# A LoRA residual kernel: the first eight tiles become two parts, and the seventh load waits for TensorE

## The chip, the cores and the metric

The kernel runs on one core of a Trainium2 chip. The metric is the device time of one execution in microseconds; the time of a kernel is the median of several executions. The kernel before takes 123.56 us (three runs, 123.53 to 123.73).

## The reference

```python
# x: (16, 512, 768) float32, A: (768, 16), B: (16, 768), scale = 0.5
lora = np.matmul(np.matmul(x, A), B)
return (x + scale * lora).astype(np.float32)
```

The rows of x are 16 * 512 = 8192 tokens of 768 numbers. Each token is projected to 16 numbers, these are raised to 768 again, scaled and added to the token. About 25 MB are read and 25 MB written.

## The kernel before, in words

**Tiles and parts.** A tile is 128 tokens, one on each of the 128 partitions of the on-chip memory: 128 rows of 3072 B, 384 KB. There are 64 tiles. `PARTS` (L14) cuts them into five parts of 8, 8, 16, 16 and 16 tiles. Within a part of S tiles, partition p holds S tokens that follow each other in memory (`memory`, L96 to L98). A transfer of all S tiles of a part is one run of memory, and each partition's piece of it is S * 3072 B long; a transfer of some of a part's tiles takes a piece out of every S * 3072 B. `x_sb` has room for 48 tiles (`ROOM`, L61), so tiles 48 to 63 take the places of tiles 0 to 15 once those have been stored (`tiles`, L103).

**Groups.** The engines work in eight groups of 8 tiles (`GROUP`). For each group:

1. ScalarE narrows tiles 0 to 3 of the group to fp16 and GpSimd tiles 4 to 7 (`narrowed`, L186 to L196, into `xn`). The first group is cut finer: tiles 0 and 1 go to GpSimd, 2 and 3 and then 4 to 7 to ScalarE. Each waits for the load that holds its tiles.
2. VectorE transposes 32x32 blocks (`turned`, L248, into `xt`).
3. TensorE projects the group with 24 matmuls (`projected`, L278 to L291, `MMS` = 24, into `ps_yt`).
4. ScalarE copies and scales the projection into a block diagonal `y_bd` (L236 to L239).
5. TensorE raises pairs of tiles (`raised`, L293 to L310, into `lora_ps`), and VectorE adds each pair to x in place (`summed`, L252 to L259, line L255, into `x_sb`).

TensorE runs a loop over the groups: raised(0), raised(1) of group g, the first 12 matmuls of the projection of group g+1, raised(2), raised(3) of group g, the last 12 matmuls of the projection. ScalarE narrows its half of group g+1 ahead of copying the projection of group g.

**SyncE issues every transfer, in an order written out by hand** (`on_sync`, L135 to L182), all on one DMA queue:

- loads 0 and 1 (tiles 0 and 1, then 2 to 7, both pieces of the first part of 8), A in three pieces, B, then loads 2 to 5 (tiles 8 to 47);
- a wait until groups 0 and 1 are summed and until the tenth pair has been raised (`s_lora`, L169); then store 0 (tiles 0 to 7) and store 1 (tiles 8 to 15), L170 and L171;
- a wait until store 0 has landed (L172), then load 6 (tiles 48 to 55, into the places of 0 to 7); a wait until store 1 has landed (L174), then load 7 (tiles 56 to 63);
- for each of the last three parts of 16 tiles a wait for its sums, then its store. The first of these also waits for the sixth group's first raise (`s_raise`, L181).

A DMA over 128 partitions has 16 engines to run on. It counts its semaphore up by 16 when it has landed, 1 for each engine that is done. `STORES` (L128) lists the stores, and `STORED` (L130) the group after which each may go.

Of the kernel before, what the change touches and what calls it, by code (L numbers as in the profile page):

```python
# [10 lines left out]

PARTS = [8, 8, 16, 16, 16]  # L14


GROUP = 8
# [11 lines left out]
def kernel(  # L29
# [8 lines left out]
    nc = tc.nc  # L38
# [9 lines left out]
    NC = D // 64  # L48
    NG = sum(PARTS) // GROUP
    PAIRS = GROUP // 2  # L50
    assert sum(PARTS) * P == T and NG * GROUP == sum(PARTS)
    sc = float(scale)


    def sb(name, shape, dtype):
        return nc.alloc_sbuf_tensor(name, shape, dtype).ap()
# [3 lines left out]

    ROOM = sum(PARTS[:-1])  # L61
    x_all = sb("x_sb", [P, ROOM, D], fp32)
# [20 lines left out]
    def sem(name):  # L83
        sems.append(nc.alloc_semaphore(name))
        return sems[-1]
# [4 lines left out]
    tok = 0  # L90
    for i, S in enumerate(PARTS):
        parts.append(tok)
# [3 lines left out]
    def memory(t2, i, s, n):  # L96
        S = PARTS[i]
        return t2[ds(parts[i], S * P), :].rearrange("(p s) d -> p s d", s=S)[:, ds(s, n), :]  # L98

    def held(i, s, n):  # L100
        return tiles(where.index((i, s)), n)

    def tiles(t, n):  # L103
        return x_all[:, ds(t % ROOM, n), :]

    LOADS = [
        (0, 0, 2), (0, 2, 6), (1, 0, 8), (2, 0, 8), (2, 8, 8), (3, 0, 16), (4, 0, 8), (4, 8, 8)
    ]
    s_load = [sem(f"s_load{k}") for k in range(len(LOADS))]

# [10 lines left out]

    s_free = [sem(f"s_free{p}") for p in range(PAIRS)]
    s_out0, s_out1, s_raise = sem("s_out0"), sem("s_out1"), sem("s_raise")

    s_sum, s_out = sem("s_sum"), sem("s_out")

    MMS = 2 * NC
    STORES = [(0, 0, 8), (1, 0, 8), (2, 0, 16), (3, 0, 16), (4, 0, 16)]  # L128

    STORED = [where.index((i, s + n - 1)) // GROUP for i, s, n in STORES]  # L130

    section = ExitStack()
    section.enter_context(tc.tile_critical(no_gpsimd_drain=True))  # L133

    def on_sync(e):  # L135
        def load(k):
            ld = LOADS[k]
            e.dma_start(out=held(*ld), in_=memory(x2, *ld)).then_inc(s_load[k], 16)  # L138

        def summed(k):  # L140
            e.wait_ge(s_sum, k + 1)
            if STORED[k] + 1 < NG:

                e.sem_inc(s_free[PAIRS - 1], 1)

        def store(k, done):
            st = STORES[k]
            e.dma_start(out=memory(out2, *st), in_=held(*st)).then_inc(done, 16)

        load(0)  # L150
        load(1)
        e.wait_ge(s_ready, 1)
        blocks = A.rearrange("(c e) r -> c (e r)", e=64)
        for c in range(SETS):
            e.dma_start(
                out=a_rows[c : SET * SET : SET, :], in_=blocks[ds(c * SET, SET), :]
            ).then_inc(s_a, 16)
        e.wait_ge(s_brows, 1)
        e.dma_start(out=b_rows[0 : R * APART : APART, :], in_=B).then_inc(s_b, 16)
        for k in range(2, len(LOADS) - 2):  # L160
            load(k)

        for p in range(2, PAIRS):
            e.sem_inc(s_free[p], 1)
        summed(0)
        summed(1)


        e.wait_ge(s_lora, 2 * PAIRS + 2)  # L169
        store(0, s_out0)  # L170
        store(1, s_out1)  # L171
        e.wait_ge(s_out0, 16)  # L172
        load(len(LOADS) - 2)
        e.wait_ge(s_out1, 16)  # L174
        load(len(LOADS) - 1)
        for k in range(2, len(STORES)):
            summed(k)
            if k == 2:


                e.wait_ge(s_raise, 6)  # L181
            store(k, s_out)  # L182

    here = set()

# [55 lines left out]
    def on_vector(e):  # L241
# [10 lines left out]
        def summed(g, p):  # L252
            xs = tiles(g * GROUP + 2 * p, 2)
            e.wait_ge(s_lora, g * PAIRS + p + 1)
            ins = e.tensor_tensor(out=xs, in0=xs, in1=lora[p % 2], op=mybir.AluOpType.add)  # L255
            if p + 1 == PAIRS and g in STORED:
                ins.then_inc(s_sum, 1)
# [15 lines left out]
    def on_tensor(e):  # L273


        xv = xt.rearrange("p s (c j k) -> p s c j k", c=NC, k=2)

        def projected(first, last):  # L278
            for m in range(first, last):
                c, k = divmod(m, 2)  # L280
                mm = e.matmul(  # L281
                    y_ps, w_bd[:, c, k, :], xv[:, :, c, :, k],
                    start=(m == 0), stop=(m == MMS - 1),
                )
                if m == 0:
                    mm.then_inc(s_turned, -1)
                if m == 1:

                    mm.then_inc(s_taken, 1)
                if m == MMS - 1:  # L290
                    mm.then_inc(s_y, 1)  # L291

        def raised(p):  # L293
            if p == 0:
                e.wait_ge(s_spread, 1)
            free = s_free[(p + 2) % PAIRS]
            e.wait_ge(free, 1)
            t = lora[p % 2]
            mms = []
            for k in range(2):  # L300
                for n0, w in ((0, 512), (512, 256)) if k == 0 else ((0, 256), (256, 512)):
                    mms.append(e.matmul(  # L302
                        t[:, k, ds(n0, w)], y_bd[:, 2 * p + k, :], b_mm[:, ds(n0, w)],
                        start=True, stop=True,
                    ))
            if p == 0:
                mms[0].then_inc(s_raise, 1)
                mms[2].then_inc(s_spread, -1)
            mms[1].then_inc(free, -1)
            mms[-1].then_inc(s_lora, 1)  # L310

        e.wait_ge(s_pick, 2)
        e.wait_ge(s_bh, 1)
        for n0, w in ((0, 512), (512, 256)):
            last = e.matmul(  # L315
                lora[0][:, 0, ds(n0, w)], pick.rearrange("p b r -> p (b r)"),
                b_half[:, ds(n0, w)], start=True, stop=True,
            )
        last.then_inc(s_bp, 1)
        e.wait_ge(s_w, 1 + NQ)  # L320
        e.wait_ge(s_turned, 1)
        projected(0, MMS)
        e.wait_ge(s_bm, 1)
        with e.Fori(0, NG - 1):
            raised(0)
            raised(1)
            e.wait_ge(s_turned, 1)
            projected(0, MMS // 2)
            raised(2)
            raised(3)  # L330
            projected(MMS // 2, MMS)
        for p in range(PAIRS):
            raised(p)

    on_sync(nc.sync)
    on_gpsimd(nc.gpsimd)
    on_scalar(nc.scalar)
# [5 lines left out]

    nc.gpsimd.wait_ge(s_sum, len(STORED))
    nc.gpsimd.sem_clear(range(nums[0], s_sum.num))
    nc.gpsimd.wait_ge(s_out, (len(STORES) - 2) * 16)
    nc.gpsimd.sem_clear(range(s_sum.num, s_out.num + 1))
    section.close()

# [34 lines left out]
```

## Time and profile before

| what | value |
|---|---|
| median of three runs | 123.56 us |
| the profiled execution: its time | 123.76 us |
| its span, from the first to the last instruction | 121.9 us |
| outside the span | 1.9 us |
| DMA queue: packets' time as a share of 16 engines' span | 96.8% |
| busy: VectorE, TensorE, ScalarE, GpSimd | 81.7, 50.5, 37.4, 28.4 us |
| read and written | 25.26 and 25.17 MB, 414 GB/s over the span |

The page cuts the span into 40 slices of 3.05 us. Its line "DMA" gives the mean busy share of the 16 DMA engines in each slice, in tenths, and its line "GB/s" what they moved. A transfer stands three times in the trace: as the instruction of SyncE that issues it, as the packets that its engines move (start, length and size of each), and as the 16 counts of its semaphore, called its landing here. One packet is one partition's piece of a transfer: 3072 B for each tile in it. Landings show how far the 16 engines are apart. Packets don't name their engine.

### The profile page before, as it was taken

The numbers are of one execution on the slowest core, as the hardware profiler recorded it, in microseconds if no ns is written. First come the engines' busy times: TensorE is split into PE (matmuls) and PEld (weight loads), VectorE is DVE, ScalarE is ACT, GpSimd is POOL, SyncE is SP. The second block draws the span as 40 slices with busy tenths as digits, with TensorE's granted clock in tenths as the row PEclk, the third lists the DMA queues.
The fourth block names the chain that finished last, engine by engine and source line by source line (L and its number), as shares of the span: only waits on it lengthen the run. The fifth ranks groups of instructions, "written<-read, shape, count | busy, mean of one in ns | idle before, by whom it ended". The sixth has DMA issues, their size and how long they took to land.

```text
span 121.9 us, 885 instructions
## 1 busy us (share of the span) xinstructions
PE 50.5 (41%) x322; PEld 29.3 (24%) x322; DVE 81.7 (67%) x42; ACT 37.4 (31%) x43; POOL 28.4 (23%) x24
## 2 busy tenths in 40 slices
PE   0000239487457457647756714774674320000000
PEld 0000026244233233424424402442442110000000
DVE  0003850799999999999999959999995991000000
ACT  4003929444426402917230093643004000000000
POOL 7732638044026002607100090630000000000000
PEclk9999999999999999999999999999999985555555
DMA  3999999999997996999989999998998999899890
GB/s 67 421 429 429 443 443 403 451 435 419 476 516 339 435 516 298 460 403 443 443 363 460 427 427 468 451 484 387 419 500 387 403 516 403 371 516 419 355 516 0
DMA packets 1928, 50.43 MB, mean 414 GB/s; under 512 B 236, under 2 KB 236, under 8 KB 392
## 3 DMA queue, kind: packets, MB, share of 16 engines
q1 hardware_dynamic: 1928, 50.43, 96.8%
HBM read 25.26 MB, written 25.17 MB: 414 GB/s over the span
## 4 chain that ended last, share of the span: by engine, by line
DVE 33%; DMA 29%; PE 9%; ACT 6%; POOL 2%; issue 2%; SPq 0%; DVEq 0%
DVE x_sb L255 21%; DMA x_sb<-in_x_dram 20%; DVE xt L250 12%; DMA out_dram<-x_sb 9%; PE ps_yt L281 6%; ACT xn L194 3%; PE lora_ps L302 3%; ACT y_bd L238 2%; POOL xn L194 2%; SPq L138 0%; SPq L379 0%; DVEq L268 0%; SPq L133 0%
## 5 line engine op out<-in xcount | busy, mean ns | idle before, releaser
L255 DVE TENSOR_TENSOR x_sb<-x_sb,lora_ps 128x1536 f32<-128x1536 f32 x32 | 53.7, 1735 | 1.4 <-PE lora_ps L302 1.4
L302 PE MATMUL lora_ps<-b_mm,y_bd 128*128 128x512 f16 (+1 forms) x128 | 25.1, 328 | 23.7 <-ACT y_bd L238 15.3
L194 ACT CAST xn<-x_sb 128x3072 f16<-128x3072 f32 (+1 forms) x9 | 23.4, 2609 | 37.2 <-DMA x_sb<-in_x_dram 28.0
L250 DVE STREAM_TRANSPOSE xt<-xn 128x3072 f32<-128x3072 f32 (+1 forms) x9 | 27.0, 3005 | 6.7 <-PE ps_yt L281 4.9
L194 POOL CAST xn<-x_sb 128x3072 f16<-128x3072 f32 (+1 forms) x8 | 20.7, 2588 | 45.3 <-DMA x_sb<-in_x_dram 28.6
L281 PE MATMUL ps_yt<-xt,w_bd 128*128 128x256 f16 x192 | 25.7, 285 | 11.9 <-DVE xt L250 11.9
L281 PEld LDWEIGHTS ps_yt<-xt,w_bd 128*128 128x128 f16 x192 | 18.7, 100 | 19.6 <-issue 15.0
L302 PEld LDWEIGHTS lora_ps<-b_mm,y_bd 128*128 128x128 f16 x128 | 10.5, 97 | 36.8 <-ACT y_bd L238 17.5
L238 ACT ACTIVATE y_bd<-ps_yt 32x256 f16<-32x256 f32 x32 | 12.0, 374 | 17.7 <-PE ps_yt L281 17.4
L243 DVE STREAM_TRANSPOSE a_t<-a_rows 32x1024 f32<-32x1024 f32 x1 | 1.9, 1945 | 11.2 <-DMA a_rows<-in_A_dram 11.2
L315 PE MATMUL lora_ps<-b_half,pick 128*128 128x512 f16 (+1 forms) x2 | 0.8, 500 | 12.5 <-POOL b_half L212 12.5
L315 PEld LDWEIGHTS lora_ps<-b_half,pick 128*128 128x128 f16 x2 | 0.1, 105 | 12.5 <-issue 12.5
L220 POOL COPY w_bd<-w_one 32x384 f16<-32x384 f16 x4 | 2.0, 501 | 0.2
L212 POOL CAST b_half<-b_rows 128x768 f16<-128x768 f32 x1 | 0.8, 830 | 4.5 <-DMA b_rows<-in_B_dram 4.5
L194 ACT ACT_TABLE_LOAD x1 | 1.3, 1283 | 0.9 <-SPq L133 0.9
L202 POOL MEMSET w_bd<- 128x1536 f32 x1 | 1.4, 1372 | 0.0
L199 POOL MEMSET a_rows<- 32x1024 f32 x1 | 0.9, 941 | 0.5 <-SPq L133 0.5
L214 POOL CAST w_one<-a_t 32x384 f16<-32x384 f32 x1 | 0.8, 847 | 0.9 <-DVE a_t L243 0.9
L231 ACT CAST b_mm<-lora_ps 128x768 f16<-128x768 f32 x1 | 0.8, 798 | 0.0
L200 POOL MEMSET b_rows<- 128x768 f32 x1 | 0.7, 727 | 0.0
L203 POOL MEMSET y_bd<- 128x512 f32 x1 | 0.5, 514 | 0.0
L205 POOL TENSOR_SCALAR_AFFINE_SELECT pick<-pick 128x128 f16<-128x128 f16 x1 | 0.3, 300 | 0.0
(5 smaller groups left out, 0.6 us busy)
## 6 DMA issues: line engine op xcount, KB each, us to landing
out_dram<-x_sb SPq DMA_DIRECT2D x3, 6144.0 KB, 20.0
x_sb<-in_x_dram SPq DMA_DIRECT2D x5, 3072.0 KB, 14.8
x_sb<-in_x_dram SPq DMA_DIRECT2D x1, 6144.0 KB, 41.9
out_dram<-x_sb SPq DMA_DIRECT2D x2, 3072.0 KB, 14.9
x_sb<-in_x_dram SPq DMA_DIRECT2D x1, 2304.0 KB, 9.7
x_sb<-in_x_dram SPq DMA_DIRECT2D x1, 768.0 KB, 4.5
a_rows<-in_A_dram SPq DMA_DIRECT2D x3, 16.0 KB
b_rows<-in_B_dram SPq DMA_DIRECT2D x1, 48.0 KB, 7.4
```

What stands on the lines that cost most here:

```text
L194: ins = copy(out=xn[:, ds(first, n), :], in_=tiles(t, n))
L199: e.memset(a_rows[0:Q], 0.0).then_inc(s_ready, 1)
L202: e.memset(w_bd.rearrange("p c k m -> p (c k m)").bitcast(fp32), 0.0)
L212: e.tensor_copy(out=b_half, in_=b_rows).then_inc(s_bh, 1)
L220: e.tensor_copy(out=w_bd[ds(b * Q, Q), :, :, ds(b * Q, R)], in_=w_one).then_inc(s_w, 1)
L238: last = e.mul(out=y_bd[q, :, q], in_=y_ps[q, :, :], mul=sc)
L243: e.transpose(out=a_t[0:Q].rearrange("i k r c -> i (k r) c"), in_=a_rows[0:Q].rearrange("c (i k r) -> c (k r) i", k=2, r=R),).then_inc(s_r ...
L250: return e.transpose(out=ts[0], in_=ts[1])
L255: ins = e.tensor_tensor(out=xs, in0=xs, in1=lora[p % 2], op=mybir.AluOpType.add)
L281: mm = e.matmul(y_ps, w_bd[:, c, k, :], xv[:, :, c, :, k], start=(m == 0), stop=(m == MMS - 1),)
L302: mms.append(e.matmul(t[:, k, ds(n0, w)], y_bd[:, 2 * p + k, :], b_mm[:, ds(n0, w)], start=True, stop=True,))
L315: last = e.matmul(lora[0][:, 0, ds(n0, w)], pick.rearrange("p b r -> p (b r)"), b_half[:, ds(n0, w)], start=True, stop=True,)
```

## The change

The first part of 8 tiles becomes two parts of 2 and 6 tiles, so that each of the first two loads is one run of memory and not 128 pieces out of a longer one. Tokens 0 to 255 are then tiles 0 and 1, and tokens 256 to 1023 are tiles 2 to 7. The store of 8 tiles becomes two: the 6 tiles first, then the 2, both counting one semaphore to 32. Load 6 waits for both, and then also for a new semaphore, `s_part`, to reach 5: TensorE counts it up at the twenty-first of the 24 matmuls of every projection (m == 20), so it reaches 5 near the end of the fifth group's projection. The rest of the order, and the instructions of all engines but SyncE, stay as they are; the lists are renumbered for the added part.

```diff
-PARTS = [8, 8, 16, 16, 16]
+PARTS = [2, 6, 8, 16, 16, 16]
...
     LOADS = [
-        (0, 0, 2), (0, 2, 6), (1, 0, 8), (2, 0, 8), (2, 8, 8), (3, 0, 16), (4, 0, 8), (4, 8, 8)
+        (0, 0, 2), (1, 0, 6), (2, 0, 8), (3, 0, 8), (3, 8, 8), (4, 0, 16), (5, 0, 8), (5, 8, 8)
     ]
...
-    STORES = [(0, 0, 8), (1, 0, 8), (2, 0, 16), (3, 0, 16), (4, 0, 16)]
+    STORES = [(1, 0, 6), (0, 0, 2), (2, 0, 8), (3, 0, 16), (4, 0, 16), (5, 0, 16)]
     STORED = [where.index((i, s + n - 1)) // GROUP for i, s, n in STORES]
+    assert STORED[0] == STORED[1]
+    STORED = STORED[1:]
...
         e.wait_ge(s_lora, 2 * PAIRS + 2)
         store(0, s_out0)
-        store(1, s_out1)
-        e.wait_ge(s_out0, 16)
+        store(1, s_out0)
+        store(2, s_out1)
+        e.wait_ge(s_out0, 32)
+        e.wait_ge(s_part, 5)
         load(len(LOADS) - 2)
         e.wait_ge(s_out1, 16)
         load(len(LOADS) - 1)
-        for k in range(2, len(STORES)):
+        for k in range(2, len(STORED)):
             summed(k)
             if k == 2:
                 e.wait_ge(s_raise, 6)
-            store(k, s_out)
+            store(k + 1, s_out)
...
                 if m == 1:
                     mm.then_inc(s_taken, 1)
+                if m == MMS - 4:
+                    mm.then_inc(s_part, 1)
                 if m == MMS - 1:
                     mm.then_inc(s_y, 1)
```

More of the change, by code (lines that the diff above doesn't have):

```diff
@@ L123 @@
     s_out0, s_out1, s_raise = sem("s_out0"), sem("s_out1"), sem("s_raise")
+    s_part = sem("s_part")
     s_sum, s_out = sem("s_sum"), sem("s_out")
     MMS = 2 * NC
-    STORES = [(0, 0, 8), (1, 0, 8), (2, 0, 16), (3, 0, 16), (4, 0, 16)]
+    STORES = [(1, 0, 6), (0, 0, 2), (2, 0, 8), (3, 0, 16), (4, 0, 16), (5, 0, 16)]
     STORED = [where.index((i, s + n - 1)) // GROUP for i, s, n in STORES]
+    assert STORED[0] == STORED[1]
+    STORED = STORED[1:]
     section = ExitStack()
@@ L345 @@
     nc.gpsimd.sem_clear(range(nums[0], s_sum.num))
-    nc.gpsimd.wait_ge(s_out, (len(STORES) - 2) * 16)
+    nc.gpsimd.wait_ge(s_out, (len(STORES) - 3) * 16)
     nc.gpsimd.sem_clear(range(s_sum.num, s_out.num + 1))
```

## The prediction

> **What bounds the kernel now.** I read the page's parts 2 and 3 first. These are the lines of the DMA engines, of the traffic, and of the queue:
>
> ```profile
> DMA  3999999999997996999989999998998999899890
> GB/s 67 421 429 429 443 443 403 451 435 419 476 516 339 435 516 298 460 403 443 443 363 460 427 427 468 451 484 387 419 500 387 403 516 403 371 516 419 355 516 0
> DMA packets 1928, 50.43 MB, mean 414 GB/s; under 512 B 236, under 2 KB 236, under 8 KB 392
> q1 hardware_dynamic: 1928, 50.43, 96.8%
> ```
>
> The 16 DMA engines are busy from the first slice to the last but one. Only the first 2.0 us (first packet 1.99) and some 3 us at the end hold no data. VectorE, the busiest other engine, adds its last pair at 101.0 us, and store 3 still moves until 106.5 (its landing), so the engines have 5 us to spare. The time is packets, divided by 16 engines, plus whatever makes the **slowest DMA engine** stand still.
>
> Next I asked for SyncE's waits and its timeline, since SyncE issues everything:
>
> ```profile
> SPq L138 <- DMA out_dram<-x_sb: 17.6, 2, 10.5
> ```
> ```profile
> 43.92 0.82 SPq L148 DMA_DIRECT2D out_dram<-x_sb  x2
> 55.30 7.74 SPq L138 DMA_DIRECT2D x_sb<-in_x_dram  x2
> 74.87 26.51 SPq L148 DMA_DIRECT2D out_dram<-x_sb  x3
> ```
>
> Stores 0 and 1 go out at 43.92, load 6 at 55.30 when store 0 has landed, load 7 at 62.70 when store 1 has, store 2 at 74.87. The landings (16 counts each, first and last) are: load 5 46.99 and 48.00, store 0 54.32 and 55.28, store 1 62.23 and 62.68, load 6 69.08 and 70.06, load 7 76.38 and 77.38, store 4 119.85 and 121.03. So the queue works in order, each 8 tiles take 7.3 us, and load 6 stands queued for 5 to 7 us behind store 1. The last landing is 1.18 us behind the first: that spread is what can be won inside the stream.
>
> Where it comes from, the windows around the hand-overs show (DMA share and GB/s are the last two columns):
>
> ```profile
> 46.00:48.00 2.00, 1.66 (x12) 0.79 (x9) 2.00 (x2) 0.00 (x0) 0.00 (x0) 1.00 0.72 307
> 60.00:64.00 4.00, 2.28 (x14) 0.91 (x12) 4.00 (x3) 1.50 (x4) 0.00 (x0) 1.00 0.94 375
> 76.00:78.00 2.00, 1.50 (x12) 1.08 (x12) 2.00 (x3) 0.60 (x1) 0.57 (x1) 1.00 1.20 516
> 62.70:70.10 7.40, 5.23 (x37) 3.01 (x35) 7.40 (x5) 0.02 (x1) 0.00 (x0) 1.00 1.00 428
> ```
>
> A steady stretch moves 428 to 431 GB/s, and 60 to 64 moved 375. (Two-us windows sway with 48 KB packets, so I take the packets themselves.) A 24,576 B packet takes 912 ns nearly always. Of store 1's last packets six took 1161 to 1722 ns, 249 to 810 too long; then three of load 6's first took 1114, 1114 and 1366, 200 to 454 too long. At load 5 to store 0 two of load 5's last 49,152 B packets lost 439 and 466 ns. At load 7 to store 2 no packet lost over 40 ns.
>
> These losses last. Load 6's landings are eleven from 69.08 to 69.60 and five from 69.83 to 70.06; those of store 4 are ten from 119.85 to 120.33 and six from 120.58 to 121.03. By their packets' ends, two of load 6's late five are the ones delayed at load 5, the other three those delayed at load 6's own first packets.
>
> **The change part by part.**
>
> *Loads 0 and 1 as runs of memory.* The packets stay 6144 and 18,432 B, as many as before, on the same engines. Load 2 is a run of memory already and moves 24,576 B in 912 ns, 37.1 ns per KB of 1000 B; load 1, in pieces, takes 686 ns for 18,432 B, 37.2. No gain there. Load 0's packets take 234 ns at best and 310 on average; over 8 packets an engine that is 0.6 us lost, at the start of a cold stream. If that is the pieces' fault, up to 0.6 us goes; if the rows' closeness hurts, as much may come. I take 0, since load 1's pieces cost nothing.
>
> *The store of 8 as 6 and 2.* Per engine, eight packets of 912 ns (and 4 between packets) become eight of 686 and eight of 234, with one more count of 9: 8 * (690 + 238) + 13 - 8 * 916 = 109 ns. DMA is the bound, so **+0.11 us**, with nothing that hides it. SyncE's third issue takes 0.33 to 0.43 us (the range of its five stores) and pushes store 1's issue from 44.3 to 44.7. Load 5 keeps the engines until 47, so this costs nothing; without that cover it would cost those 0.4 us.
>
> [...]
>
> *The order, six tiles ahead of two, and their joint semaphore* move nothing: both land before store 1, near 55.4.
>
> *The wait on TensorE.* The fifth projection's second half is this row of TensorE's timeline:
>
> ```profile
> 59.13 1.50 PE L281 MATMUL ps_yt<-xt,w_bd 128*128 128x256 f16 x12
> ```
>
> m == 20 is the ninth of these 12: 59.13 + 9 * 0.125 = 60.25. VectorE paces that row and is busy throughout from 25 to 70, so it stays. Load 6 is issued at 60.25 and no longer at 55.30. Behind it SyncE holds the wait for store 1 (until 62.7) and load 7, which aren't delayed. At the start of the kernel 1.02 us lay between an issue (0.97) and its first packet (1.99); so load 6's packets can start at 61.3. Store 1's engines get through it between 61.1 (without its stalls) and 62.2, and 0.11 later with the split. The queue just does not run dry, or does by 0.1 us on the earliest engine, which isn't the slowest.
>
> What this does to the stall, no row shows. Its bounds: it stays (0) or goes. If it goes, the latest engine is one of those delayed at load 5: their landings of store 4 are 120.58 and 120.61 in place of 121.03, **-0.43 us**. A new stall as large again is the bound above, +0.45. I take -0.43, by the nearest rows: the three hand-overs between loads and stores lost more, the longer the next transfer had stood in the queue. It was issued 1.5 to 2.5 us before the landings at load 7 to store 2 (no packet over 40 ns late), 3.1 to 4.1 at load 5 to store 0 (two packets late by 0.45), 7 at store 1 to load 6 (nine). With the change it is 2.0 to 2.4.
>
> Load 6 lands about 0.3 earlier, load 7 and store 2's issue (casts, scaling and the sixth raise follow load 6) move with it.
>
> **The sum.** 0 + 0.11 - 0.43 = -0.32 us. On the profiled execution: 123.76 - 0.32 = 123.44. That one stood 0.20 over the median of the runs; from the median, 123.56 - 0.32 = **123.24 us**.
>
> **The rivals.**
>
> *The stall belongs to the turn from stores to loads, whenever the load was issued.* For it: it is the only hand-over from a store to a load, and the only one with six late packets. Against it: load 5 to store 0 has the same kind of stall the other way. Only the split remains: 123.56 + 0.11 = 123.67.
>
> *The queue runs dry, slower than before.* Load 0 took 3.66 us from issue (0.97) to its first landing (4.63), 1.76 more than its eight packets of 238 ns. If load 6 needs that much before it flows, it flows from 60.25 + 1.76 = 62.0 at best, and 62.9 by load 0's last landing (5.52, 0.9 later). The slowest engine is through store 1 at 62.3. From that point each us costs one us: 123.56 + 0.11 + 0.6 = 124.27. Against it: the first packet itself came after 1.02 us, and store 2, issued 1.5 us ahead of load 7's first landing, cost nothing.
>
> The Trainium skill (DMA: Bandwidth & Descriptors, "Rules for kernel authors") says to issue a DMA early so that its setup overlaps with work; it is on this rival's side, and no run here shows the limit.
>
> *More goes than I took:* the start's 0.6 us in part, or the stall at load 5 too, since the stores' shape there changes. Then the latest engine is one of the main ten (120.33): 123.56 - 0.70 + 0.11 = 122.97, and less if the start gains.
>
> **How the numbers follow.** Forecast 0.45, stall remains 0.28, dry queue 0.17, more gain 0.10. 0.2% is 0.25 us, about what a measurement of this kernel can tell from no change: faster is below 123.31, slower above 123.81. The forecast is near that limit and some of it falls within; some of the remaining stall, with a start that loses, falls above. Faster 0.50, same 0.29, slower 0.21. The range reaches from the larger gain to the middle of the dry queue's prices, 122.85 to 124.05.
>
> **What would show it.** Right: load 6's issue near 60.25, no store packet of 24,576 B over 1000 ns around 61 us, load 6's landings with three fewer late ones, store 4's last landing 0.3 us earlier. Store 0's two parts 0.11 us longer than 7.33. Wrong: an idle DMA between 61 and 63; load 6's issue past 61; late packets still there; or a start whose load 0 lands 0.3 us off 4.63 to 5.52.

## The result, and the profile after

The changed kernel takes **125.09 us** (median of eight runs, 124.18 to 125.80) against 123.64 us for the kernel before (eight runs beside it, 123.47 to 123.85). The ratio is 1.0109, with a 95% interval of 1.0075 to 1.0143: 1.1% slower. The runs of the changed kernel lie 1.6 us apart, those of the kernel before 0.4. Ratios here leave out executions more than 1.5% above the fastest of their kernel, which matters most in run 4.

The profiled execution of the changed kernel took 124.98 us, its span 123.2. The lines of the page that answer to those of before (busy tenths of the DMA engines and GB/s in 40 slices, here of 3.08 us; packets; the queue):

```profile
DMA  3999999999999988999899999998999999899890
GB/s 94 437 437 421 439 447 415 423 447 431 463 431 511 415 351 377 413 447 471 335 343 415 463 399 399 535 431 383 463 447 415 415 479 447 351 495 431 351 511 0
DMA packets 2072, 50.43 MB, mean 409 GB/s; under 512 B 252, under 2 KB 252, under 8 KB 536
q1 hardware_dynamic: 2072, 50.43, 96.4%
```

The busy share hardly moves, 96.8 to 96.4%, though 1.2 us were added to the span. A packet that crawls is busy all the same, so this share can't show the loss. GB/s can: slices 19 and 20 (counted from 0; 58.5 to 64.7 us) moved 335 and 343, and in the kernel before no two neighbouring slices are that low.

SyncE's waits and timeline of the changed kernel:

```profile
SPq L180 <- PE ps_yt L289: 14.8, 1, 14.8
...
SPq L142 <- DMA out_dram<-x_sb: 2.0, 1, 2.0
```
```profile
44.12 1.57 SPq L152 DMA_DIRECT2D out_dram<-x_sb  x3
60.58 2.74 SPq L142 DMA_DIRECT2D x_sb<-in_x_dram  x2
76.19 26.71 SPq L152 DMA_DIRECT2D out_dram<-x_sb  x3
```

Load 6 now waits for TensorE (L180) and goes out at 60.58, 5.3 us later than before; load 7 follows when store 1 has landed. Store 2 goes out 1.3 us later, since its chain starts at load 6's landing.

One microsecond at a time around the hand-over from store 1 to load 6 (DMA share and GB/s are last), first before, then after:

```profile
61.00:62.00 1.00, 0.00 (x0) 0.00 (x0) 1.00 (x2) 0.96 (x4) 0.00 (x0) 1.00 0.75 320
62.00:63.00 1.00, 0.75 (x4) 0.31 (x4) 1.00 (x1) 0.20 (x1) 0.00 (x0) 1.00 0.97 393
...
60.00:66.00 6.00, 3.10 (x22) 1.66 (x21) 6.00 (x4) 1.50 (x4) 0.00 (x0) 1.00 0.96 393
```
```profile
61.00:62.00 1.00, 0.00 (x0) 0.00 (x0) 1.00 (x2) 0.98 (x3) 0.00 (x0) 1.00 1.21 320
62.00:63.00 1.00, 0.55 (x4) 0.31 (x4) 1.00 (x1) 0.38 (x2) 0.00 (x0) 1.00 0.61 172
...
60.00:66.00 6.00, 3.10 (x22) 1.68 (x20) 6.00 (x4) 1.50 (x4) 0.00 (x0) 1.00 0.95 348
```

The six us moved 348 GB/s and not 393. A packet's time and its bytes are both counted where it starts, so single microseconds swing; the sum over six tells more. At 6 us * 45 GB/s, 270 KB were missing, 0.63 us of a steady stream.

From the packets I work out two numbers for a stretch, each a mean over the 16 engines: **idle**, in which an engine holds no packet, and **late**, the time by which packets exceed the usual length of their size (912 ns for 24,576 B, 1815 for 49,152, 686 for 18,432, 234 for 6144). A value down to -0.06 for idle is zero, since neighbouring packets overlap by some ns.

| stretch (us) | before: idle, late | after: idle, late | after less before |
|---|---|---|---|
| 2 to 6, start | 0.32, 0.63 | 0.22, 0.42 | -0.31 |
| 42 to 50, load 5 to store 0 | -0.02, 0.09 | -0.03, 0.22 | +0.13 |
| 59.5 to 66.5, store 1 to load 6 | -0.02, 0.27 | 0.36, 0.84 | **+0.95** |
| 74 to 81, load 7 to store 2 | -0.02, 0.02 | 0.11, 0.04 | +0.16 |
| 88 to 119 | -0.06, 0.03 | -0.07, 0.11 | +0.07 |

With the 0.11 of the split the sum is 1.1. Store 4's landings, in mean over the 16, came at 121.46 and not at 120.39: +1.07. So the time is found, and most of it, in net, at one hand-over. Load 6 landed 1.10 later (71.16 for 70.06).

What changed there is worth a look. In the kernel before, store 1's last packets were late, six of them by 249 to 810 ns. In the changed one none of store 1's is late by over 50 ns, and 14 of load 6's first sixteen are, by 66 to 1457 ns, and eight more behind them by over 60.

### The profile page after: what moved, and what is told of

Read it like the earlier page. It is cut to its first block, busy times and chain, and to the rows that moved or that the text cites. A ratio compares the mean times of both kernels' runs of the same rounds, so it can differ in the third digit from the quotient of the medians.

```text
span 123.2 us, 887 instructions
## 1 busy us (share of the span) xinstructions
PE 52.3 (42%) x322; PEld 30.5 (25%) x322; DVE 81.8 (66%) x42; ACT 37.5 (30%) x43; POOL 28.4 (23%) x24
## 3 DMA queue, kind: packets, MB, share of 16 engines
q1 hardware_dynamic: 2072, 50.43, 96.4%
## 4 chain that ended last, share of the span: by engine, by line
DVE 42%; DMA 16%; PE 13%; ACT 8%; issue 3%; SPq 0%
DVE x_sb L263 27%; DMA x_sb<-in_x_dram 16%; DVE xt L258 15%; PE ps_yt L289 8%; ACT xn L202 6%; PE lora_ps L312 5%; ACT y_bd L246 2%; SPq L142 0%; SPq L389 0%; SPq L137 0%; SPq L180 0%
## 5 line engine op out<-in xcount | busy, mean ns | idle before, releaser
L312 PE MATMUL lora_ps<-b_mm,y_bd 128*128 128x512 f16 (+1 forms) x128 | 26.2, 340 | 24.0 <-ACT y_bd L246 16.4
L289 PE MATMUL ps_yt<-xt,w_bd 128*128 128x256 f16 x192 | 26.8, 293 | 11.5 <-DVE xt L258 11.5
L289 PEld LDWEIGHTS ps_yt<-xt,w_bd 128*128 128x128 f16 x192 | 19.4, 103 | 19.7 <-issue 14.5
```

The lines of the kernel that those rows point to most:

```text
L289: mm = e.matmul(y_ps, w_bd[:, c, k, :], xv[:, :, c, :, k], start=(m == 0), stop=(m == MMS - 1),)
L312: mms.append(e.matmul(t[:, k, ds(n0, w)], y_bd[:, 2 * p + k, :], b_mm[:, ds(n0, w)], start=True, stop=True,))
```

## The experiments

Theory, formed from this: a load that reaches the engines only when they run out of packets starts slowly, like load 0 at the kernel's start. Rival: the cut store or the closer rows cost the time, and the wait only shifts it.

**1. The wait alone, in the kernel before.**

```diff
         e.wait_ge(s_out0, 16)
+        e.wait_ge(s_part, 5)
         load(len(LOADS) - 2)
...
+                if m == MMS - 4:
+                    mm.then_inc(s_part, 1)
```

> The kernel before with only the wait of load 6 on the fifth projection (issue near 60.5 in place of 55.3); parts, loads and stores as before. Theory (a load that is issued only some 1 to 2 us before the stores ahead of it end has its first packets delayed, as load 0's were at the start): nearly the whole loss, +0.8 to +1.4 us, ratio 1.007 to 1.011, 10 or more packets of load 6 over 1000 ns after 61.5. Rival (the split of the store, or the closer rows, is what costs): within 0.3 us of before.

Measured: 124.99 us, ratio 1.0108 (1.0085 to 1.0131), the whole loss. Load 6 went out at 60.92; the hand-over cost 0.57 idle and 0.80 late. The windows of this kernel:

```profile
61.00:62.00 1.00, 0.16 (x2) 0.00 (x0) 1.00 (x1) 0.78 (x3) 0.00 (x0) 1.00 0.73 148
62.00:63.00 1.00, 0.21 (x1) 0.11 (x2) 1.00 (x2) 0.72 (x2) 0.00 (x0) 1.00 0.82 221
63.00:64.00 1.00, 1.00 (x8) 0.59 (x6) 1.00 (x1) 0.00 (x0) 0.00 (x0) 1.00 0.81 319
...
60.00:66.00 6.00, 2.92 (x22) 1.75 (x20) 6.00 (x4) 1.50 (x4) 0.00 (x0) 1.00 0.87 315
```

Three us in a row moved 148, 221 and 319 GB/s, and the six 315 in place of 393, without any cut store.

**2. The change without the wait**, and **3. the cut store alone** (the part of 8 kept, its tiles 2 to 7 stored first).

```diff
-        e.wait_ge(s_part, 5)
```

> The changed kernel without the wait on the fifth projection: parts of 2 and 6, two stores, load 6 issued when both have landed (near 55.7). Theory (the late issue costs): +0.1 to +0.4 us, since the split alone adds 0.11 by packets; ratio 1.000 to 1.003. Rival (split or rows cost): +0.9 us or more.

```diff
-    STORES = [(0, 0, 8), (1, 0, 8), (2, 0, 16), (3, 0, 16), (4, 0, 16)]
+    STORES = [(0, 2, 6), (0, 0, 2), (1, 0, 8), (2, 0, 16), (3, 0, 16), (4, 0, 16)]
...
-        store(1, s_out1)
-        e.wait_ge(s_out0, 16)
+        store(1, s_out0)
+        store(2, s_out1)
+        e.wait_ge(s_out0, 32)
```

> The kernel before with the store of 8 tiles cut into 6 and 2 (in pieces of the part of 8, loads as before), load 6 waiting for both stores, no other wait. Theory: +0.1 to +0.2 us, by packets. Rival (a further DMA in the queue disturbs the hand-over from load 5): +0.4 us or more, with load 5's last packets more delayed than before.

Measured: 123.79 us, 1.0011 (0.9996 to 1.0027), and 123.82 us, 1.0012 (0.9999 to 1.0024). Both fit what the split's packets cost, and neither is clear of no change. In their traces the hand-over to load 6 cost 0.20 and 0.15. The rival falls: the wait makes the loss, the rest next to none.

**4. Another load issued late: load 5, behind load 4** (`s_part` counted as in run 1).

```diff
-        for k in range(2, len(LOADS) - 2):
+        for k in range(2, len(LOADS) - 3):
             load(k)
         for p in range(2, PAIRS):
             e.sem_inc(s_free[p], 1)
+        e.wait_ge(s_part, 2)
+        load(len(LOADS) - 3)
```

> The kernel before with load 5 (16 tiles) issued only at the second projection's end, near 30.4, some 2 us before load 4 lands; it was issued at the start. Here the queue turns from a load to a load. Theory A (any load that is issued late starts with slow packets): load 5's first packets over 1000 ns more than one by one, +0.5 to +1 us. Theory B (the stall needs the turn from stores to loads, late issue only makes it worse): within 0.2 us of before, load 5's first packets at 1815 to 1830 ns.

Measured: 123.62 to 127.63 us, ratio 1.0058 (1.0029 to 1.0087); the median of all twelve executions is 125.57. The trace is of one at 126.11, which the ratio leaves out, so I take from it only where its time went. Load 5 was issued at 31.21, 1.3 us before load 4's first landing. All 16 of its first packets were late, by 130 to 1216 ns: 0.32 idle and 0.62 late between 31 and 36, against none in the kernel before. No store is near, so a late load needs no turn from stores to start slowly: theory A, in this one trace. More was lost later in it: 0.79 of late packets at load 5's end, and 0.73 idle before a late store 2, whose own packets were hardly late (0.04).

**5 to 7. How late is late?** Load 6 behind the fifteenth, sixteenth or seventeenth raised pair in place of `s_part`:

```diff
         e.wait_ge(s_out0, 16)
+        e.wait_ge(s_lora, 15)     # 16, 17
         load(len(LOADS) - 2)
```

> The kernel before with load 6 also waiting for the fifteenth raised pair: issue near 57.7, some 3.4 us before the earliest engine is through store 1 (61.1). Theory T (threshold: only a load whose packets aren't yet queued when an engine runs out starts slowly, which takes 1 to 1.5 us after the issue): within 0.15 us of before. Rival G (gradual: the later the issue, the slower the start): +0.3 to +0.7 us.

> The same with the sixteenth raised pair: issue near 59.3, 1.8 us before the earliest engine is through store 1. T: within 0.25 us of before, with 0 to 3 more late packets. G: +0.6 to +1.0 us.

> The same with the seventeenth raised pair: issue near 63.1, after store 1 has landed (62.7), so the queue surely runs dry. Both T and G: the wait alone lost 1.35 us at an issue of 60.9; here 2.2 us later, with engines free between 61.1 and 62.2, so 1.35 plus at most 2.2: +2.5 to +3.6 us, every engine's first packet of load 6 starting after 64.0. If the slow start and the dry time overlap, +1.8 to +2.5.

| load 6 issued, in the trace | idle, late (59.5 to 66.5) | ratio |
|---|---|---|
| 55.30 (before) | -0.02, 0.27 | 1 |
| 58.37 (fifteenth) | -0.04, 0.20 | 1.0004 (0.9996 to 1.0013) |
| 59.01 (sixteenth) | -0.04, 0.04 | 1.0088 (1.0060 to 1.0117) |
| 60.92 (the wait alone) | 0.57, 0.80 | 1.0108 (1.0085 to 1.0131) |
| 62.99 (seventeenth) | 2.30, 0.85 | 1.0330 (1.0299 to 1.0361) |

The first engine was through store 1 between 61.1 and 61.5 in these traces. The load queued 2.7 us ahead of that (fifteenth) cost nothing; those whose packets came after it (wait alone, seventeenth) cost the idle time and 0.8 us of slow packets on top. The windows of the seventeenth show both apart:

```profile
62.00:63.00 1.00, 0.82 (x4) 0.31 (x4) 1.00 (x1) 0.02 (x1) 0.00 (x0) 1.00 0.00 0
63.00:64.00 1.00, 0.08 (x1) 0.08 (x2) 1.00 (x1) 0.00 (x0) 0.00 (x0) 1.00 0.73 147
64.00:65.00 1.00, 0.76 (x5) 0.27 (x6) 1.00 (x2) 0.00 (x0) 0.00 (x0) 1.00 0.99 246
65.00:66.00 1.00, 1.00 (x10) 0.85 (x11) 1.00 (x1) 0.00 (x0) 0.00 (x0) 1.00 0.68 295
```

First a microsecond with nothing, then three at 147 to 295 GB/s though packets are there. Nothing else moves data meanwhile, so this is the loads' own start.

The sixteenth doesn't fit: its trace, of its fastest run, is clean at load 6. So I took another.

**12. The same kernel again, for its trace.**

> The kernel with load 6 at the sixteenth raised pair once more, for a second trace: the first, at 123.93, was the fastest of six (to 125.24) and issued load 6 at 59.01, with no slow start. Theory T with a threshold near 2 us: a run near 124.5 shows its issue at 59.3 or later and idle or slow first packets of load 6, 0.4 us or more in mean. Rival: the time goes at load 5's end (0.44 us of late packets in the first trace), and load 6 starts clean again.

It took 123.82 us, issued load 6 at 59.17 and was clean there again (-0.03, 0.06). Its runs before had gone up to 125.24. The issue's time follows the engines' work, which over all traces lies up to 1.1 us apart (store 0 went out from 43.43 to 44.56 behind the same raised pair), so runs with the issue near 60 are likely among them; no trace of one was taken, and it stays argued. The other candidate is load 5's end, which lost 0.44 and 0.27 us in the two traces and 0.09 in the kernel before.

**8 and 9. Stores 0 and 1, earlier and later.** For the hand-over from load 5 to store 0 the prediction had the rule that a longer queue loses more.

```diff
-        e.wait_ge(s_lora, 2 * PAIRS + 2)      # 8: without it; 9: s_taken at 4 in its place
```

> The kernel before without SyncE's wait for the tenth raised pair: stores 0 and 1 issued when group 1 is summed, near 42, 5 to 6 us ahead of load 5's landings and not 3 to 4. The prediction's rule (the longer a transfer stands queued, the more is lost at the hand-over): more late packets at load 5's end than two, +0.2 to +0.5 us. Theory (a late issue costs, an early one doesn't): within 0.2 us of before, or up to 0.3 us less.

> The kernel before with stores 0 and 1 issued when the fourth projection has begun, near 45.6 in place of 43.9. Over the traces so far the time that packets lost around load 5's end falls as stores 0 and 1 are issued later: 0.79 us (mean of 16 engines) at 41.97, 0.78 at 43.43, 0.44 at 43.54, 0.32 at 43.74, 0.09 at 43.92, 0.02 at 44.46 and 44.56. Theory (an early store disturbs the load that still runs): late packets under 0.05 us; but the first packets come at 46.6, when the earliest engines run out, so 0 to 0.3 us of idle time. Together -0.2 to +0.3 us against before. Theory that stores start slowly when issued late, as loads do: +0.8 us or more.

Earlier (issue 41.97): 124.16 us, 1.0039 (1.0026 to 1.0052). My new theory expected no loss and missed; the prediction's rule held for stores: 19 packets of load 5 were late, 0.79 us in mean. Later (issue 46.03): 124.63 us, 1.0089 (1.0074 to 1.0103), also missed. Load 5's end was quiet (0.03 idle, 0.04 late), but now store 1's last packets, before a load 6 issued early at 55.24, were late on all 16 engines, 0.71 us in mean (0.83 over the whole stretch). Here all engines came to the end of store 1 within 0.4 us, in step (their last packets began at 60.70 to 61.09). So a turn from stores to a queued load can cost as much as a late load. Is the late issue then only harmful because it makes the engines start in step?

**13. The wait, where the engines come apart.** The early stores of run 8, in which the hand-over to load 6 cost only 0.02, with the wait of run 1. In its trace store 0 went out at 42.77, and the engines' last packets of store 1 began 0.94 us apart, against 0.49 in run 1.

> Stores 0 and 1 issued early (near 42, as in the run that lost 0.79 us at load 5's end and only 0.02 at load 6's start), and load 6 waiting for the fifth projection (near 60.6). Late issue costs by itself (dry queue): idle and slow first packets of load 6 of 0.8 to 1.4 us in mean, the time 0.9 to 1.5 us above that run's 124.16: 125.1 to 125.7. Only engines in step lose: 0.3 us or less there, 124.2 to 124.5.

Measured: 125.68 us, 1.0164 (1.0133 to 1.0196); issue 61.16, 0.28 idle and 0.98 late, with all 16 first packets of load 6 late. The late issue costs by itself.

**14. A quarter of load 6 queued early** (`s_part` again as in run 1).

```diff
-        (0, 0, 2), (0, 2, 6), (1, 0, 8), (2, 0, 8), (2, 8, 8), (3, 0, 16), (4, 0, 8), (4, 8, 8)
+        (0, 0, 2), (0, 2, 6), (1, 0, 8), (2, 0, 8), (2, 8, 8), (3, 0, 16), (4, 0, 2), (4, 2, 6), (4, 8, 8)
...
-        for k in range(2, len(LOADS) - 2):
+        for k in range(2, len(LOADS) - 3):
...
+        load(len(LOADS) - 3)
+        e.wait_ge(s_part, 5)
         load(len(LOADS) - 2)
```

> The kernel before with load 6 cut: its first 2 tiles issued at 55.3 when store 0 has landed, its other 6 only at the fifth projection (near 60.5 to 61). The 2 tiles give each engine 1.85 us of packets. Dry queue as the cause: no idle time, and the 6 tiles' first packets near 730 ns and less; within 0.3 us of before (the split costs 0.1). If issuing a load while store 1 ends disturbs by itself, whatever is queued: the loss of the wait alone, +1.0 to +1.4 us, stays.

Measured: 123.87 us, 1.0027 (1.0012 to 1.0043), ten runs from 123.62 to 124.41. The hand-over is clean, -0.06 idle and 0.06 late; of the packets there only three are late by over 50 ns, by 183 to 307. Its windows, to be read beside those of run 1:

```profile
61.00:62.00 1.00, 0.21 (x1) 0.11 (x2) 1.00 (x2) 0.72 (x2) 0.00 (x0) 1.00 0.59 246
62.00:63.00 1.00, 0.61 (x4) 0.20 (x2) 1.00 (x1) 0.00 (x0) 0.00 (x0) 1.00 0.95 399
63.00:64.00 1.00, 0.67 (x4) 0.31 (x4) 1.00 (x1) 0.00 (x0) 0.00 (x0) 1.00 1.15 485
...
60.00:66.00 6.00, 2.79 (x19) 1.50 (x18) 6.00 (x3) 1.50 (x4) 0.00 (x0) 1.00 0.96 407
```

The 6 tiles went out at 59.86 in the trace, and their packets began at 63.30, behind the two tiles. The wait is the same as in run 1; what differs is that the engines had a load queued when the store ended. (The trace's issue is 1.06 us earlier than in run 1's, by the spread told at run 12; but all ten executions lie below the fastest of run 1, 124.71.) So a **dry queue** is the cause. The remaining 0.33 us is more than the 0.1 of one more cut; this trace lost 0.39 at load 5's end, where the kernel before lost 0.09.

**10 and 11. A better version?** Stores 0 and 1 some 0.5 us later, by twelve increments of an unused semaphore on SyncE, in the kernel before, and in the changed kernel without its wait.

```diff
         e.wait_ge(s_lora, 2 * PAIRS + 2)
+        for _ in range(12):
+            e.sem_inc(s_tick, 1)
```

> The kernel before with twelve increments of an unused semaphore on SyncE ahead of store 0, some 0.5 us later (near 44.4 to 44.9). Theory as above: -0.1 to -0.3 us, the late packets at load 5's end under 0.05 us in mean. If the loss there only moves by chance from run to run: within 0.15 us of before.

> The changed kernel without the wait on the fifth projection and with those twelve increments. Traces of kernels with the closer rows lost 0.59 and 0.64 us (idle and late, mean of 16 engines, 2 to 6 us) at the start, those without 0.84 to 0.99: -0.3; the split +0.11; the quieter end of load 5 -0.1 to -0.3. Theory: -0.2 to -0.5 us against before. If the start's gain is lost in the spread between engines: within 0.2 us.

Measured: 123.65 us, 1.0002 (0.9992 to 1.0012), and 123.60 us, 1.0008 (0.9992 to 1.0024). Both expectations missed: no gain. In run 10 load 5's end lost 0.04, but one engine ended 0.76 us behind the other 15 (landings of store 4: 119.95 to 120.39, then 121.15). No version beat the kernel before.

## Why the prediction was wrong

*The bound* was right: every microsecond found is a DMA engine idle or slow.

*Loads as runs of memory*, taken at 0 with 0.6 either way: three traces with the closer rows lost 0.5 to 0.6 us in the first stretch (idle and late), thirteen without 0.85 to 1.0. So the cold start gains 0.3 us in mean, which the time doesn't show: with the rows 1.0011, without 1.0012. The landings of load 0 fit that: their mean is 4.74 for 5.14, but the last is 5.46 for 5.52, so the slowest engine gained little.

*The cut store*, +0.11: measured 0.15 (0.0012 * 123.64), interval -0.01 to 0.30. The term fits, though no cost at all would nearly fit too.

*The wait* is the step that failed, in two places. The first: "The queue just does not run dry, or does by 0.1 us on the earliest engine, which isn't the slowest." Load 6's issue (60.58 for 60.25) and first packet (61.57 for 61.3) came 0.3 us later than forecast, and the engines were through store 1 sooner. Store 1's counts began at 60.98, where I had 61.1 and 0.11 more, and came in mean at 61.54, against 61.83 in the kernel before. Of these 0.29 us, 0.21 are the hold-up of six last packets, which is gone; the start's gain, which I had put at 0, is the likely reason for the earliest engine, but no run shows it alone. So nine of the 16 engines were through by 61.33, ahead of the first packet, and not the earliest alone. Idle: 0.36.

The second is the term of -0.43, by the rule that a hand-over loses more the longer the next transfer stood queued. The rule mixed two things that came from three rows. For a store behind a load it holds (run 8: 0.79 at 41.97). For a load it was the other way round: queued early its cost was 0.27 (though 0.83 in run 9), late 0.84 and idle on top. The late store packets did vanish, as forecast; load 6's first packets took their place. In all that is +0.95 in place of -0.43, and store 2, whose chain hangs on load 6's landing, came too late as well (idle 0.11 at 74 to 81, which I had moving along at no cost).

*The rival of the dry queue* was the mechanism, at a chance of 0.17, and it had named load 0's slow start as the price. Its 124.27 was too low by 0.8: I charged only the slowest engine's wait for the first full flow (0.6), where load 6's first packets crawl on all engines, after the gap and on top of it.

The Trainium skill (DMA: Bandwidth & Descriptors, "Rules for kernel authors") says to issue DMAs early so that their setup overlaps. For loads these runs agree (1.0108 with load 6 late, 1.0004 at 58.37). For stores they do not: issued 1.95 us earlier (41.97 for 43.92), ratio 1.0039.

## What to carry to other kernels

In a stream that the DMA engines bound, a wait ahead of a load is safe only if the queue still holds enough work when the wait ends (run 5, with 2.7 us of it, lost nothing), and a load that finds the queue dry pays for the gap and for a slow start. When estimating when a queue runs out, do it for every engine, without the stalls that the change itself removes and with what it gains earlier. Busy share hides slow packets; read GB/s and packet lengths.

## What the hardware showed that I had not expected

- Loads into a dry queue start slowly: 0.8 to 1.0 us in mean over 16 engines for their first packets (24,576 B in up to 2800 ns for 912), four times over, after stores (runs 1, 7, 13 and the changed kernel); 0.62 after a load (run 4, one trace). A store that comes late costs its gap alone: 0.04 late at store 2 both in the changed kernel (0.11 idle) and in run 4 (0.73 idle). What makes a load's first packets slow no run here shows.
- Stores issued behind a running load slow the load's last packets, on the whole the more the earlier: 0.79 us at an issue of 41.97, 0.44 at 43.54, 0.32 at 43.74, 0.27 at 43.70, 0.09 at 43.92, 0.02 to 0.04 at 44.45 to 44.56 and at 46.03. It isn't strict: 0.39 at 42.77 (run 13) and at 43.46 (run 14), and with three stores 0.78 at 43.43, 0.22 at 44.12, 0.02 at 44.35 and 0.16 at 44.37. (Load 5 of run 4, late itself, is left out.) Why, and why the hand-over to a load 6 queued early cost 0.83 us in run 9, stays open.
